# A two-layer GDN and HGRN2 flow step on one core: padded decay operands, token-tile order at the norms, key norms from the Gram diagonal, and a new plan

## The chip, the cores and the metric

The kernel runs on one core of a Trainium2 chip. The metric is the time of one execution on the device in microseconds (us). The time before is the median of three runs; the profile belongs to a fourth execution of the same kernel.

## The reference, cut to what matters

Two layers of a bidirectional backbone run on 128 prompt tokens and 256 sample tokens with D = 1024 and 8 heads of 128. Layer a mixes with a gated delta rule (GDN), layer b with HGRN2; after each mixer comes an MLP with 4096 hidden units. All weights and activations are fp32.

```
for layer in range(2):
    hmod = rms_norm(x, norm_g[layer, 0]) * (1 + sc1) + sh1
    mix  = gated_deltanet_mixer(hmod) if layer == 0 else hgrn2_mixer(hmod)
    x    = x + gt1 * rms_norm(mix, norm_g[layer, 1])
    hmod = rms_norm(x, norm_g[layer, 2]) * (1 + sc2) + sh2
    ff   = square(relu(hmod @ mlp_w1[layer])) @ mlp_w2[layer]
    x    = x + gt2 * rms_norm(ff, norm_g[layer, 3])

# inside the GDN mixer, per head, direction and chunk of 64 tokens
k      = k * rsqrt(sum(k * k) + 1e-6)
g      = cumsum(g)
decay  = exp(where(causal, g[i] - g[j], -inf))
lower  = (k * beta) @ k.T * decay * strict
tmat   = inverse(eye + lower)
u, w   = tmat @ (v * beta), tmat @ (k * beta * exp(g))
v_new  = u - w @ state
state  = state * exp(g_last) + (k * exp(g_last - g)).T @ v_new
```

sh1, sc1, gt1, sh2, sc2 and gt2 are six rows of silu(c) @ w_ada + b_ada, one set for the prompt and one for the sample.

## The kernel before, in words

The 384 tokens are three token tiles of 128: n = 0 is the prompt, n = 1 and 2 the sample. Activations stand transposed, 128 features by 384 tokens per tile. An fp32 product is made of three matmuls (`mm3`): both operands are split into a rounded high part and the rest, so every weight piece of 128x1024 goes through `split` (L1013): ACT writes wh, a rounded copy, and DVE writes wl, the difference. Both are in classes of three buffers. Matmuls go through the helper line L924, transposes through L930, DMAs through L941, DVE's tensor_tensor through L838, its scalar_tensor_tensor through L843, its tensor_scalar through L849, ACT's activations through L887 and its copies through L892, memsets through L856.

The order of the instructions is not that of the code. `Planner` (L540) records every operation with its unit (for instance d3 for the decay of head 3), and `run` (L625) then makes a list schedule of all five queues with estimated costs. The tables RESERVE, SHIFT, ADA and BUFS and the numbers SWITCH and WINDOW weight that choice; CAPS bounds the buffers of each class (L4, of tiles with up to 4 KB a row, has 9; L3, of 3 KB, has 4). A matmul whose operand shape differs from the one before is charged 85 ns there, a DMA 2000 ns of latency and its bytes at 320 per ns. Each engine then executes its list in order, and SP issues all DMAs in one order.

The steps that the change touches:

- **Gates and decays** (`gdn`, L1345, from the rows of `gp` on; `decay`, L1468). The cumulated log gates are cut into three bf16 parts (`gp`), stored to DRAM (`gd`) and loaded back into two tiles LH and RH of class L4 (tag LR), in rows 32n to 32n+5 for token tile n; the memsets of the two tiles give the ones and minus ones. `decay(h)` makes, for each of 8 heads and 3 token tiles, one PSUM tile of 128x256 out of three matmuls: maskb against identb (128 rows), then for both directions a product over 6 rows of LH and RH. ACT takes the exponential into `dec` (class L3), and one DMA stores the 384 KB of a head to `dd`.
- **Key norms** (`phase1`, L1504). The Gram matrix of a token tile's keys is in PSUM (pk). ACT squares the keys (k2), three matmuls against a column of ones (cst) give their sums, DVE's `c` and `iv` and POOL's `vsc` follow, and six DVE operations PU = pk * gam * dec give the matrix that `inverse` (L1536) inverts for four heads at a time. Four heads' PU go through DRAM (`du`) into the 31 steps of substitution and back (`dt`), and `merge` (L1579) puts 32x32 blocks together.
- **State step** (`vstep`, L1653). ACT writes w = py * gam out of PSUM, DVE multiplies w by a decay, and the product goes into the state matmul.
- **Borders.** `out_proj` (L1197, for both layers) and the last group of `w2` in `mlp` (L1284) accumulate three token tiles (acc) over pieces of the weights. `postnorm` (L1172) of a token tile follows when its last piece is in, then `prenorm` (L1147) of the next stage: ACT's sqj, POOL's rstd, DVE's pnt, x and xn, transposes (pj<-sml,xn), ACT's hhi and DVE's hlo, and only then the next stage's matmuls. In all of them the loop over pieces is outside the loop over token tiles.
- **First HGRN head** (`head`, L1760): its f and i products (pf) run over pieces outside, token tiles inside, too.

Other loads that run through the GDN stage are the rows of w_ada: ar (512 KB each, multiplied on TensorE into pad) and av (512 KB each, multiplied on DVE into avj with cvec, the broadcast condition).

Of the kernel before, what the change touches and what calls it, by code (L numbers as in the profile page):

```python
# [34 lines left out]
RESERVE = {'A32': 39,  # L35
 'A64': 69,
 'CR': 12,
 'HC': 5,
 'LR': 1,
 'PU': 16,  # L40
 'T64': 19,
 'Zs': 24,
 'ab': 15,
 'acc': 2,
 'adw': 0,
 'am': 25,
 'ar': 2,
 'atm': 56,
 'att': 7,
 'av': 2,  # L50
 'avj': 0,
 'ax': 3,
 'c1': 31,
 'cacc': 0,
 'cb': 3,
 'cbuf': 2,
 'crow': 42,
 'cvec': 2,
 'dec': 15,
 'dre': 20,  # L60
 'e1': 41,
 'gate': 4,
 'gp': 17,
 'gr': 10,
 'hE': 8,
 'hEn': 20,
 'hKD': 7,
 'hQD': 3,
 'hel': 27,
 'het': 2,  # L70
 'hf': 7,
 'hf0': 0,
 'hhi': 33,
 'hk': 15,
 'hlo': 23,
 'hsf': 5,
 'inv': 10,
 'iv': 33,
 'k0': 8,
 'k2': 0,  # L80
 'kT': 29,
 'ktt': 2,
 'lbo': 2,
 'lhl': 20,
 'mh': 29,
 'ml': 34,
 'mr': 8,
 'mst': 18,
 'nat': 2,
 'natr': 12,  # L90
 'of': 0,
 'ofl': 1,
 'oin': 45,
 'on': 64,
 'ors': 22,
 'osb': 0,
 'pad': 2,
 'pb': 2,
 'pf': 1,
 'pj': 2,  # L100
 'pm': 6,
 'pnt': 9,
 'po': 0,
 'qT': 1,
 'r': 42,
 'rstd': 32,
 'rsu': 34,
 's0': 3,
 's1': 73,
 'sf': 2,  # L110
 'sg': 16,
 'sqj': 0,
 'ss': 23,
 'ss2': 30,
 'sso': 37,
 'ssq': 28,
 'swt': 2,
 'tb': 1,
 'th': 3,
 'vT': 1,  # L120
 'vtt': 1,
 'w': 59,
 'w2': 61,
 'wh': 0,
 'wl': 0,
 'wr': 31,
 'x': 11,
 'xn': 28,
 'zl': 0,
 'zs': 3}  # L130
SWITCH = 862
TICK = 10240 / 3
WINDOW = 3068
SHIFT = {'aoh0': 4453,
 'aopn0': -32,
 'aopn1': -26,
 'aopn2': 55,
 'aow0': 3100,
 'aow1': -316,
 'aow2': 1579,  # L140
 'aow3': 201,
 'aow:ld': 826,
 'aow:sp': 2736,
 'apost0': 1380,
 'apost1': 184,
 'apost2': 4855,
 'apre0': 9298,
 'apre1': 6920,
 'apre2': 760,
 'awi0': 34,  # L150
 'awi1': -119,
 'awi2': 381,
 'awi3': 2862,
 'awi4': 1676,
 'awi5': 528,
 'awi6': 4228,
 'awi7': 770,
 'awi:ld': 3909,
 'awi:sp': 2021,
 'awo0': 5745,  # L160
 'awo1': 5025,
 'awo2': 14621,
 'awo3': 1449,
 'awo4': 4497,
 'awo5': 1510,
 'awo6': 1868,
 'awo7': 8060,
 'awo:ld': 5382,
 'awo:sp': 8906,
 'boh0': 3541,  # L170
 'bopn0': 5070,
 'bopn1': 3053,
 'bopn2': 4485,
 'bow0': -479,
 'bow1': -142,
 'bow2': 4668,
 'bow3': 10062,
 'bow:ld': 10903,
 'bow:sp': 2510,
 'bpost0': 318,  # L180
 'bpost1': -325,
 'bpost2': -72,
 'bpre0': 9493,
 'bpre1': 2181,
 'bpre2': 7646,
 'bwi0': -84,
# [1898 lines left out]
```

## Time and profile before

| | us |
|---|---|
| median of three runs | 1237.83 (1234.85 to 1239.44) |
| profiled execution | 1235.33 |
| its span | 1233.3 |
| PE busy | 1180.0 (96%) |
| DVE busy | 800.2 (65%) |
| ACT busy | 635.4 (52%) |
| POOL busy | 66.1 (5%) |
| moved by DMA | 207.82 MB |

The profiled execution is 2.50 us under the median, 0.2%. The mean granted clock of TensorE is 0.966 of full speed. Reading by stage: 0 to 87 us are the first norms, k projections and gates of layer a; 87 to 118 the decays; 118 to 176 projections beside the first inverse; 176 to 365 the merges, the heads' cores and the output projection; 390 to 650 the first MLP; 663 to 943 HGRN2; 962 to 1220 the second MLP. The short stretches between are the borders, where a norm stands between two products.

### The profile page before, as it was taken

What the parts mean: (1) busy time and instruction counts of PE and PEld (TensorE: products, weight loads), DVE (VectorE), ACT (ScalarE), POOL (GpSimd) and SP (SyncE); (2) the same over time, 40 slices, a digit from 0 to 9 for tenths busy, and PEclk for the clock granted to TensorE, in tenths of its full rate; (3) what the DMA queues carried; (4) which work ended last, traced back from release to release, by engine and by line L of the source; (5) the groups of instructions that cost most, each with busy time, mean ns of one, the idle gap of its engine ahead of it and who ended that gap; (6) DMA issues with size and microseconds to landing.
All of it is one profiled execution on the core that took longest, in us unless ns stands there. A gap on an engine that the chain in (4) does not pass through costs nothing.

```text
span 1233.3 us, 20383 instructions
## 1 busy us (share of the span) xinstructions
PE 1180.0 (96%) x7936; PEld 1047.6 (85%) x7936; DVE 800.2 (65%) x1578; ACT 635.4 (52%) x1283; POOL 66.1 (5%) x156
## 2 busy tenths in 40 slices
PE   6998998999998999999998999999998999999997
PEld 3775988888987998989988998888986999888986
DVE  4484878867999986666539967767666542333334
ACT  3383464775646643343436567674655564333442
POOL 1111001000002000000002000000002000000000
PEclk9996996899998999999998999999999999999999
DMA  9868771675353875556436642233432334233432
GB/s 359 318 248 281 225 214 33 198 248 186 119 182 134 302 237 191 192 184 205 152 115 205 210 150 97 76 110 111 159 133 84 107 137 137 103 127 118 138 129 86
DMA packets 82642, 207.82 MB, mean 169 GB/s; under 512 B 26058, under 2 KB 47842, under 8 KB 70514
## 3 DMA queue, kind: packets, MB, share of 16 engines
q1 hardware_dynamic: 82546, 206.53, 49.4%
q8 instruction: 62, 1.02, 0.3%
q14 instruction: 34, 0.28, 0.1%
HBM read 192.52 MB, written 13.99 MB: 167 GB/s over the span
## 4 chain that ended last, share of the span: by engine, by line
PE 60%; DVE 7%; ACT 5%; issue 2%; POOL 1%; POOLq 0%; DVEq 0%; ACTq 0%
PE acc L924 24%; PE pj L924 21%; PE pf L924 7%; PE nat L924 3%; PE pb L924 2%; PE po L924 1%; DVE wl L838 1%; ACT L887 1%; DVE A L838 1%; POOL rstd L838 1%; PE pb L930 1%; PE pj L930 1%; ACT wh L892 1%; DVE avj L843 1%; DVE hQD L838 1%
## 5 line engine op out<-in xcount | busy, mean ns | idle before, releaser
L838 DVE TENSOR_TENSOR wl<-wr,wh 128x1024 fp32r<-128x1024 f32 (+2 forms) x228 | 266.6, 1171 | 268.1 <-ACT wh L892 260.1
L892 ACT CAST wh<-wr 128x1024 fp32r<-128x1024 f32 (+2 forms) x228 | 230.3, 1010 | 403.8 <-PE pj L924 178.0
L924 PE MATMUL pj<-hhi,wh 128*128 128x384 f32 x800 | 272.5, 343 | 0.0
L924 PE MATMUL pj<-hhi,wl 128*128 128x384 f32 x800 | 271.1, 342 | 0.0
L924 PE MATMUL pj<-hlo,wh 128*128 128x384 f32 x800 | 270.9, 341 | 0.0
L924 PEld LDWEIGHTS pj<-hhi,wh 128*128 128x128 f32 x800 | 151.6, 190 | 2.4 <-issue 0.8
L924 PEld LDWEIGHTS pj<-hlo,wh 128*128 128x128 f32 x800 | 151.5, 190 | 1.8 <-issue 0.4
L924 PEld LDWEIGHTS pj<-hhi,wl 128*128 128x128 f32 x800 | 151.6, 190 | 1.4 <-DVE wl L838 0.5
L924 PE MATMUL acc<-wl,mh 128*128 128x512 f32 x384 | 149.5, 390 | 0.0
L924 PE MATMUL acc<-wh,ml 128*128 128x512 f32 x384 | 149.3, 390 | 0.0
L924 PE MATMUL acc<-wh,mh 128*128 128x512 f32 x384 | 145.4, 390 | 0.0
L843 DVE SCALAR_TENSOR_TENSOR avj<-av,cvec 128x1024 bf16<-128x1024 f32 x112 | 135.5, 1218 | 6.9 <-DMA dd<-dec 3.7
L924 PEld LDWEIGHTS acc<-wl,mh 128*128 128x128 f32 x384 | 72.1, 188 | 15.8
L924 PEld LDWEIGHTS acc<-wh,mh 128*128 128x128 f32 x384 | 72.1, 188 | 14.7
L924 PEld LDWEIGHTS acc<-wh,ml 128*128 128x128 f32 x384 | 72.1, 188 | 14.2
L924 PE MATMUL pf<-wh,hhi 128*128 128x384 f32 x192 | 63.6, 346 | 2.3 <-ACT hhi L892 2.3
L924 PE MATMUL pf<-wl,hhi 128*128 128x384 f32 x192 | 63.9, 342 | 0.1
L924 PE MATMUL pf<-wh,hlo 128*128 128x384 f32 x192 | 63.8, 345 | 0.0
L843 DVE SCALAR_TENSOR_TENSOR cacc<-cb,sml,cacc 128x392 f32<-128x392 f32 x96 | 58.9, 619 | 5.4 <-ACT cacc L887 4.5
L887 ACT ACT_TABLE_LOAD x35 | 44.9, 1283 | 3.6 <-DVE hk L849 2.4
L838 DVE TENSOR_TENSOR ml<-mr,mh 128x384 fp32r<-128x384 f32 x56 | 30.2, 554 | 14.7 <-PE acc L924 7.5
L924 PEld LDWEIGHTS pf<-wh,hhi 128*128 128x128 f32 x192 | 36.2, 190 | 2.9 <-ACT hhi L892 2.5
(255 smaller groups left out, 1898.0 us busy)
## 6 DMA issues: line engine op xcount, KB each, us to landing
wr<-in_w_dram SPq DMA_DIRECT2D x64, 1024.0 KB
av<-in_wv_dram SPq DMA_DIRECT2D x56, 512.0 KB
ar<-in_wa_dram SPq DMA_DIRECT2D x40, 512.0 KB
wr<-in_gq_dram SPq DMA_DIRECT2D x14, 1024.0 KB
wr<-in_hfi_dram SPq DMA_DIRECT2D x16, 768.0 KB
wr<-in_hqz_dram SPq DMA_DIRECT2D x8, 1024.0 KB
wr<-in_gout_dram SPq DMA_DIRECT2D x4, 1024.0 KB
wr<-in_hout_dram SPq DMA_DIRECT2D x4, 1024.0 KB
```

The lines of the kernel that those rows point to most:

```text
L838: self._go(lambda: self.r.tensor_tensor(fix(out), fix(in0), fix(in1), op), _n(out), [out], [in0, in1], rate, base=base)
L843: self._go(lambda: self.r.scalar_tensor_tensor(fix(out), fix(in0), fix(scalar), fix(in1), op0, op1, **{k: fix(v) for k, v in kw.items()}), ...
L887: self.pl.add("S", lambda: self.r.activation(fix(out), fix(in_), func, **{k: fix(v) for k, v in kw.items()}), cost, w, [x for x in (in_, b ...
L892: self.pl.add("S", lambda: self.r.copy(fix(out), fix(in_)), cost, [out], [in_])
L924: self.pl.add("PE", lambda: self.r.matmul(fix(out), lhsT=fix(lhsT), rhs=fix(rhs), start=start() if callable(start) else start, stop=stop, ...
L930: self.pl.add("PE", lambda: self.r.transpose(fix(out), fix(in_), fix(ident)), 111.0, [out], [in_, ident], geo=(4, 4))
```

## The change

**Decay operands.** LH becomes three tiles, one for each token tile, and RH one, all with 128 rows in class L4 (four buffers instead of two). Outside of its six rows an LH tile is zero; the decay matmul runs over all 128 rows. POOL makes seven memsets instead of two.

**Token-tile order.** `out_proj` for its second column half, a new `w2_last` for the last group of `w2`, and the first HGRN head's hfi split all four weight pieces first (`split4`; the fourth piece goes into class L4 under the tags xh and xl) and then finish token tile 0 over the whole sum, its postnorm, token tile 1, token tile 2.

**Key norms.** The sum of squares is read off the Gram matrix: one DVE scalar_tensor_tensor for each token tile multiplies pk by the identity and accumulates along the row. ACT's square and the three matmuls go. A product gam2 = gam * decay is made once for each head; in `vstep` DVE writes w2 = py * gam2 directly out of PSUM.

**Plan.** The shape change costs 160 ns instead of 85 in the planner, a DMA 2200 ns and its bytes run at 300 per ns; all tables are new. Class sm has four more real buffers, and two paddings (32 and 16 floats a row) stand in SBUF.

```diff
-RESERVE = {'A32': 39,
+RESERVE = {'A32': 55,
...
-SWITCH = 862
+GAP = 32
+SKEW = 16
+SWITCH = 1602
...
-                    st += 85.0
+                    st += 160.0
...
-                dma_free = max(dma_free, st + 2000.0) + op.dma
+                dma_free = max(dma_free, st + 2200.0) + op.dma
...
+    def split4(raws, shape):
+        out = []
+        for i in range(4):
+            extra = dict(cls=("L4", "L4"), tag=("xh", "xl")) if i == 3 else {}
+            out.append(split(raws[i // 2][:, 2 * (i % 2):2 * (i % 2) + 2], shape, **extra))
+        return out
...
+        pcs = split4([load(w[2 + kh], 4) for kh in range(2)], [128, 2, 512])
+        for n in range(NT):
+            pl.unit(f"{u}ow2")
+            pst[n][1] = ps("acc", 6)
+            for k in range(KC):
+                hi, lo = pcs[k // 2]
+                mm3(pst[n][1], hT["hi"][k][:, tsl[n]], hT["lo"][k][:, tsl[n]], hi[:, k % 2, :], lo[:, k % 2, :],
+                    k == 0, k == KC - 1)
+            pl.unit(f"{u}opn{n}")
+            postnorm(n, pst[n], x[n], gate)
...
+        def w2_last():
+            hh, hl = hbuf.pop(7)
+            pl.unit(f"{'ab'[l]}wo7")
+            pcs = split4([load(a["w2"][l, 14 + half], 4) for half in range(2)], [128, 2, 512])
+            for n in range(NT):
...
+                postnorm(n, [acc[n, 0], acc[n, 1]], x[n], gate, store)
...
-        LH = tl("L4", "LR", 2, [70, 16, 128], B16)
-        RH = tl("L4", "LR", 2, [70, 16, 128], B16)
-        G.memset(LH, 1.0, after=[p])
+        LH = [tl("L4", "LR", 4, [128, 16, 128], B16) for _ in range(NT)]
+        RH = tl("L4", "LR", 4, [128, 16, 128], B16)
         G.memset(RH, -1.0, after=[p])
         for n in range(NT):
             src = gd[:, :, tsl[n]].rearrange("r m t -> m r t")
-            DM.dma_start(out=LH[32 * n + 3:32 * n + 6], in_=src)
+            G.memset(LH[n], 0.0, after=[p])
+            G.memset(LH[n][32 * n:32 * n + 6], 1.0)
+            DM.dma_start(out=LH[n][32 * n + 3:32 * n + 6], in_=src)
...
-                    PE.matmul(px[:, c:c + 128], lhsT=LH[32 * n:32 * n + 6, d * 8 + h, :],
-                              rhs=RH[32 * n:32 * n + 6, d * 8 + h, :], start=False, stop=(d == 1))
+                    PE.matmul(px[:, c:c + 128], lhsT=LH[n][:, d * 8 + h, :], rhs=RH[:, d * 8 + h, :],
+                              start=False, stop=(d == 1))
...
-            k2 = tl("L1", "k2", 1, [128, T])
-            S.activation(k2, k, AF.Square)
-            pss = pb()
+            c1 = tl("sm", "c1", 2, [128, NT])
+            dj = tl("Lh", "dj", 1, [128, 128])
             for n in range(NT):
-                PE.matmul(pss[:, n:n + 1], lhsT=k2[:, tsl[n]], rhs=cst[:, C_ONE:C_ONE + 1], start=True, stop=True)
-            c1 = tl("sm", "c1", 2, [128, NT])
-            V.tensor_scalar(c1, pss[:, 0:NT], 1.0, EPS, ALU.mult, ALU.add)
+                V.scalar_tensor_tensor(dj, pk[:, tsl[n]], 1.0, ident, ALU.mult, ALU.mult, accum_out=c1[:, n:n + 1])
+            V.tensor_scalar(c1, c1, 1.0, EPS, ALU.mult, ALU.add)
...
-                    V.tensor_scalar(w2, w, EX[:, 2 + d, n, h:h + 1], None, ALU.mult)
+                    V.tensor_scalar(w2, py[:, 0:128], gam2[:, h, n, d:d + 1], None, ALU.mult)
```

How the order moves at three places. First SP's queue in the decay stage: dd is the store of a head's decays, ar and av are rows of w_ada, cvec the broadcast condition, adw and gt the result rows of w_ada, du the blocks for the inverse, s a state. Before, from the first dd on:

```order
L941 DMA dd<-dec_971 128x768
L941 DMA adw_1010<-in_adw_dram 128x512
L941 DMA ar_1020<-in_wa_dram 128x1024
L941 DMA gt_0_93<-adw_204 2x256
L941 DMA av_1033<-in_wv_dram 128x1024
L941 DMA cvec_1042<-cs 128x8x128
L941 DMA cvec_1051<-cs 128x8x128
L941 DMA dd<-dec_1065 128x768
L941 DMA dd<-dec_1084 128x768
L941 DMA av_1102<-in_wv_dram 128x1024
L941 DMA dd<-dec_1137 128x768
L941 DMA du_89<-PU_1002 32x12x32
```

And now:

```order
L952 DMA dd<-dec_972 128x768
L952 DMA dd<-dec_1000 128x768
L952 DMA ar_1027<-in_wa_dram 128x1024
L952 DMA gt_0_94<-adw_372 2x256
L952 DMA ar_1046<-in_wa_dram 128x1024
L952 DMA dd<-dec_1052 128x768
L952 DMA ar_1078<-in_wa_dram 128x1024
L952 DMA s_412_1093<-in_state_gdn_dram 128x2x128
L952 DMA dd<-dec_1080 128x768
L952 DMA du_90<-PU_996 32x12x32
L952 DMA gt_0_94<-adw_372 2x256
L952 DMA ar_1121<-in_wa_dram 128x1024
```

Both cvec and all av have left the space between the stores; some ar have come in.

Second POOL's list, from the last memset of the conv buffers (cb) before the decay operands (LR) to the first after them. Before:

```order
L856 MEMSET cb_117 128x5x2
L849 ISA
L849 TENSOR_SCALAR rsu_177<-ss_169 128x1
L838 TENSOR_TENSOR rstd_182<-rsu_177,nhalf 128x1
L849 TENSOR_SCALAR rsu_187<-ss_180 128x1
L838 TENSOR_TENSOR rstd_191<-rsu_187,nhalf 128x1
L849 TENSOR_SCALAR rsu_201<-ss_196 128x1
L838 TENSOR_TENSOR rstd_206<-rsu_201,nhalf 128x1
L856 MEMSET LR_630 70x2048
L856 MEMSET LR_649 70x2048
L856 MEMSET cb_725 128x2
```

And now:

```order
L867 MEMSET cb_198 128x5x2
L867 MEMSET LR_617 128x2048
L867 MEMSET LR_643 128x2048
L867 MEMSET LR_617 6x2048
L867 MEMSET LR_643 6x2048
L867 MEMSET LR_701 128x2048
L867 MEMSET LR_722 128x2048
L867 MEMSET LR_701 6x2048
L867 MEMSET cb_691 128x2
L867 MEMSET cb_691 128x5x2
```

Seven long memsets stand in one block ahead of the next conv buffers.

Third PE at the border from HGRN2's output projection to the second MLP: acc is the last accumulation of the projection, pj<-sml,xn a transpose of the normed tokens, nat the first product of the MLP. Before:

```order
L924 MATMUL acc_10201<-wh_10211,hlo_9865 128x512
L924 MATMUL acc_10201<-wh_10211,hhi_9861 128x512
L924 MATMUL acc_10201<-wl_10218,hhi_9861 128x512
L924 MATMUL acc_10201<-wh_10211,hlo_9865 128x512
L924 MATMUL pb_10298<-vtt_9298,het_9913 128x128 x2
L930 MATMUL pj_10303<-sml,xn_10256 128x128 x4
L924 MATMUL nat_10339<-wh_10239,hhi_10330 128x256
L924 MATMUL nat_10339<-wl_10261,hhi_10330 128x256
L924 MATMUL nat_10339<-wh_10239,hlo_10341 128x256
L930 MATMUL pj_10355<-sml,xn_10311 128x128 x4
```

And now:

```order
L935 MATMUL acc_10249<-wh_10168,hhi_9113 128x512
L935 MATMUL acc_10249<-wl_10178,hhi_9113 128x512
L941 MATMUL pj_10275<-sml,xn_10231 128x128 x4
L941 MATMUL pj_10280<-sml,xn_10231 128x128 x4
L935 MATMUL acc_10249<-wh_10168,hlo_9161 128x512
L935 MATMUL acc_10249<-wh_10168,hhi_9113 128x512
L935 MATMUL acc_10249<-wl_10178,hhi_9113 128x512
L935 MATMUL acc_10249<-wh_10168,hlo_9161 128x512
```

The transposes of token tile 0 now stand ahead of the last matmuls of the accumulation, not behind it.

## Rows read from the trace of the kernel before

**Rows 1.** Windows by stage: us, busy us of each engine (count), granted clock, DMA share, GB/s.

```profile
99.00:118.00 19.00, 15.93 (x75) 10.66 (x75) 10.82 (x31) 6.71 (x19) 3.32 (x5) 0.50 0.87 268
...
123.00:176.00 53.00, 53.00 (x319) 51.29 (x317) 47.26 (x118) 24.51 (x46) 1.14 (x5) 1.00 0.78 235
176.00:210.00 34.00, 28.49 (x402) 25.68 (x402) 24.25 (x68) 18.40 (x45) 2.07 (x6) 0.65 0.17 42
...
365.00:390.00 25.00, 19.69 (x98) 16.57 (x97) 23.93 (x44) 17.36 (x43) 7.71 (x17) 0.86 0.44 154
390.00:650.00 260.00, 260.00 (x1366) 237.54 (x1365) 173.23 (x241) 113.13 (x167) 1.32 (x6) 1.00 0.56 191
650.00:663.00 13.00, 9.06 (x43) 7.85 (x42) 12.11 (x26) 12.50 (x35) 7.55 (x14) 0.74 0.65 214
943.00:962.00 19.00, 13.51 (x68) 11.12 (x67) 17.56 (x32) 15.01 (x39) 7.83 (x16) 0.82 0.25 92
```

**Rows 2.** Timeline of PE in the decay stage: start, us, instruction, idle before and releaser.

```profile
87.12 0.28 PE L924 MATMUL pb<-maskb,identb 128*128 128x256 bf16 x1
...
87.55 0.28 PE L924 MATMUL pb<-maskb,identb 128*128 128x256 bf16 x1
...
105.11 0.37 PE L924 MATMUL pb<-maskb,identb 128*128 128x256 bf16 x1 [3.07 <-ACT dec L887]
...
118.15 0.67 PE L924 MATMUL pj<-hhi,wh 128*128 128x384 f32 x1
```

**Rows 3.** Waits between 87 and 118 us: waited for, us in total, times, longest.

```profile
ACT dec L887 <- DMA dd<-dec: 10.5, 3, 6.6
```

**Rows 4.** Timeline of SP's queue in the decay stage: issue, us, DMA.

```profile
90.53 0.33 SPq L941 DMA_DIRECT2D dd<-dec  x1
...
92.73 1.50 SPq L941 DMA_DIRECT2D cvec<-cs  x2
...
117.33 0.33 SPq L941 DMA_DIRECT2D dd<-dec  x1
```

**Rows 5.** DMA issues by group: count and KB each.

```profile
av<-in_wv_dram SPq DMA_DIRECT2D x56, 512.0 KB
...
dd<-dec SPq DMA_DIRECT2D x8, 384.0 KB
```

**Rows 6.** Tile LR, POOL's row: duration min/median/max ns, first and last start.

```profile
L856 POOL MEMSET LR<- x2: 1801/1802/1802, 54.1 to 55.9; 70x2048 bf16 x2
```

**Rows 7.** Timeline of DVE: two gate operations of one form, during and after those memsets.

```profile
56.97 0.90 DVE L849 TENSOR_SCALAR gr<-gr 64x384 f32<-64x384 f32 x1 [1.75 <-ACT gr L887]
...
64.52 0.42 DVE L849 TENSOR_SCALAR gr<-ax,nal 64x384 f32<-64x384 f32 x1
```

**Rows 8.** Timeline of PE at the last key norm, at full clock.

```profile
133.09 0.72 PE L924 MATMUL pb<-cst,k 128*128 128x1 f32 x6
```

**Rows 9.** Tile dec, DVE's row: duration ns min/median/max, first and last start.

```profile
L843 DVE SCALAR_TENSOR_TENSOR PU<-pb,gam,dec x24: 339/343/352, 90.1 to 107.5; 128x128 f32<-128x128 f32 x24
```

**Rows 10.** Tile w, ACT's row: the same columns.

```profile
L887 ACT ACTIVATE w<-pb,gam x48: 348/367/392, 195.2 to 352.8; 128x128 f32<-128x128 f32 x48
```

**Rows 11.** Timeline of PE at the three borders, the longest waits.

```profile
946.28 0.39 PE L924 MATMUL acc<-wh,hlo 128*128 128x512 f32 x1
946.50 0.39 PE L924 MATMUL acc<-wh,hhi 128*128 128x512 f32 x1
...
951.98 0.43 PE L924 MATMUL nat<-wh,hhi 128*128 128x256 f32 x1 [3.40 <-ACT hhi L892]
...
378.06 0.63 PE L930 MATMUL pj<-sml,xn 128*128 128x128 f32 x4 [4.04 <-DVE xn L849]
...
656.58 0.69 PE L924 MATMUL pf<-wh,hhi 128*128 128x384 f32 x1 [2.27 <-ACT hhi L892]
```

**Rows 12.** The costliest groups of instructions: weight splits, busy us, mean ns, idle before.

```profile
L838 DVE TENSOR_TENSOR wl<-wr,wh 128x1024 fp32r<-128x1024 f32 (+2 forms) x228 | 266.6, 1171 | 268.1 <-ACT wh L892 260.1
L892 ACT CAST wh<-wr 128x1024 fp32r<-128x1024 f32 (+2 forms) x228 | 230.3, 1010 | 403.8 <-PE pj L924 178.0
```

## Prediction before the run

> **What bounds the kernel now.** I read the windows by stage first. In the long products TensorE never pauses: 260.00 of 260 us in the first MLP, 53.00 of 53 beside the first inverse, at full clock [rows 1]. Only less work could shorten these stretches; the change takes none from the MLPs. The time to win stands in the short windows, and there in two columns, PE busy and granted clock. In 99 to 118 us, the decays, PE is busy 15.93 of 19 at a clock of 0.50, that is the lower of its two levels, 1.2 instead of 2.4 GHz; in 176 to 210, the first merges, 28.49 of 34 at 0.65; at the three borders 19.69 of 25, 9.06 of 13 and 13.51 of 19 at 0.86, 0.74 and 0.82 [rows 1].
>
> Second, the timeline of PE in the decay stage. The first decay group (maskb and two small products) starts at 87.12, the projections go on at 118.15: 31 us [rows 2] for 24 groups. Such a stage is not bound by PE: before the group at 105.11 PE stood 3.07 us waiting for ACT's dec [rows 2]. The waits say why ACT was late: its exponential waited 10.5 us, in three pieces and once 6.6, for the store dd<-dec to release a buffer [rows 3]. SP's queue says why the store was late: from the first store at 90.53 to the eighth at 117.33 [rows 4] stand, by the order of before, eight stores of 384 KB, five av, two ar and two cvec of 512 KB each, an adw of 256 KB and small ones: 8.3 MB (sizes from [rows 5] and, for ar, cvec and adw, from the shapes in the list). That in 26.8 us is 310 GB/s, where the windows show 268 in 99 to 118 [rows 1]. So the queue's bytes set the stage.
>
> Third, the borders: PE waits 4.04 us for xn, 2.27 for hhi and 3.40 for hhi in the longest pieces [rows 11]. What ends last there is the norm's chain of the first token tile, behind its accumulation.
>
> **The change part by part.** The sum is made against the profiled execution, 1235.33 us, 2.5 under the median.
>
> *Decay stage: −10.* In the new order the stores carry other company: between the first and the eighth stand four ar, one load of a state, one read-back dre of a head's decays (384 KB) and the du. With the eight stores that is 6.0 MB, 2.3 less; at 310 GB/s 7.4 us. The av and cvec still have to come, but into 123 to 176, where DMA is at a share of 0.78 [rows 1] and PE does not wait for it. I take −8. Padding: two groups in a row start 0.43 us apart [rows 2]; 512 columns take 0.22 us (two accumulation matmuls, 946.28 and 946.50 [rows 11]), so some 0.2 us of each group is change of shape, 5 us for 24. PE's waits cover most of it. What is left is that a denser stage may come back to the upper clock sooner: −2. Bounds: 0 (the inverse's or the projections' inputs are late anyway) and −18 (the waits, 10.5, go, and the half clock of 99 to 118 falls by most of its 9.5 us).
>
> *Start: −2.* By counting SP's lists, the eighth piece of the k weights stands behind 13.7 MB instead of 15.1. At the 268 GB/s of the window after [rows 1] 1.4 MB are 5 us; whether the start waits for loads to the end I can't tell, so bounds 0 and −5.
>
> *Key norms: −2 in all.* 48 matmul passes with one column go. Six of them took 0.72 us at full clock [rows 8], so 24 of them, for the four heads that lie in filled stretches, are 2.9 us; the other 24 lie in the decay stage, under its waits. ACT's eight squares go without effect; ACT has room. DVE gets 24 dj of the kind and size of PU, 0.343 us [rows 9], plus the read of an accumulator, so 9 to 10 us, and eight small products. DVE is busy 10.82 of 19 in the decays but 47.26 of 53 behind them [rows 1]. Four heads' 12 dj, some 5 us, stand on the way to the first inverse. That inverse is covered: PE has 53 us of projections. I charge +1; bounds 0 and +5.
>
> *State step: −1.* DVE's w2 no longer follows ACT's w of 0.367 us [rows 10]. Per step the serial chain loses a hop, but behind 250 us it is covered by projections. Only the first 8 steps, in the merges, can show it: 8 × 0.367 = 2.9 at best, 0 at worst.
>
> *POOL: +1.* Seven memsets of the 1.80 us kind [rows 6] replace two: 12.6 instead of 3.6 us in one block. Two conv buffers (cb_691, cb_727) stand behind them; DVE's convolutions for them may be late by up to 9 us, but the k projections ahead leave DVE other heads. Bounds 0 and +5. Here the trace speaks against the change in a second way: a gate operation on DVE that ran while POOL was setting LR took 0.90 us, its like behind the memsets 0.42 [rows 7]. The Trainium skill, "SBUF — State Buffer", section "Who interferes with whom", says that a DVE tensor_scalar or copy that takes both port pairs and a POOL instruction shut each other out for a whole instruction, the first to start winning. By that rule each such DVE operation in the block may lose up to a memset. That is a rival below.
>
> *Borders: −10.* Counting accumulation matmuls of 512 columns behind the last one of token tile 0, the lead of the first norm grows from 21 to 27 at the first border, from 24 to 36 at the second, from 25 to 45 at the third. At 0.227 us [rows 11] that is 1.4, 2.7 and 4.5 us more. The idle in the three windows is 5.3, 3.9 and 5.5; the lower clock costs about 25 × 0.14, 13 × 0.26 and 19 × 0.18, or 3.4 us each [rows 1]. The leads sum to 8.6. At the first border two avj that stood on DVE in the first norm's way are gone, and four small matmuls fill. I take −10; bounds 0 (the second token tile's chain is what waits next) and −25 (all idle and clock).
>
> *Splitting four pieces first: +1.* ACT takes 1.01 us and DVE 1.17 for a piece [rows 12]. In the new order some 15 matmuls stand between the first use of piece three and of piece four, 3.4 us; ACT needs one norm operation and the cast for it. It fits narrowly.
>
> *Paddings and the four small buffers: 0.* They add no instruction; no row tells what an address costs, and no engine waits for a buffer of class sm in the waits that I read.
>
> *New waits: +3.* A new plan leaves waits that its costs don't know. I take one of the size that the old one left, 3.07 [rows 2]; bounds −8 (merges: their idle and clock in 176 to 210 cost 5.5 and about 12) and +8.
>
> Sum: −10 −2 −2 −1 +1 −10 +1 +3 = −20, so 1215; I say 1216.
>
> **The rivals.**
>
> *A smaller gain.* The store waits go, but the first inverse, or POOL's block, then holds the merges: what is won at 118 us is idle in 176 to 210. For it: a clock of 0.65 there, so nothing covers. Against: the projections in between are worth 53 us. Only the borders and the norms pay: 1235 − 10 − 2 to 1235 − 4, so 1222 to 1231.
>
> *The port.* A DVE operation of the gates that starts under a memset ends with it. In the trace that cost 0.48 us once [rows 7]. If two of them each lose a whole memset of 1.80 us [rows 6], the first decay starts 3.6 us later, and every decay with it: about 1220. This is the case of the Trainium skill's rule named above.
>
> *A larger gain.* The decay stage keeps the upper clock (−9.5 of its half clock instead of −2) and the merges some of theirs (−5): about 1203.
>
> *No effect.* The padding and the token order do what they say, but another chain of equal length stands right behind each: hhi at the borders, where tile 0's xn was late before; the buffers of dec with ar in the queue instead of av. 1232 to 1244.
>
> *Slower: the four pieces.* At five places (two output projections, two ends of w2, the first HGRN head) no token tile can finish before the fourth piece is split. If the raw weights come just in time, PE stands for two pieces, 2 × (1.01 + 1.17) = 4.4 us [rows 12], five times: +22, and the borders win nothing: 1215 + 10 + 22 = 1247. It decides from the point where the fourth lo is ready later than about 4 us after PE has begun the third. Against it: DMA has a share of 0.25 to 0.65 at the borders [rows 1], so the weights lie there early.
>
> **How the numbers follow.** A measurement of this kernel can tell about 0.5% from no change, 6.2 us: faster is under 1231.6, slower over 1244. Forecast (1208 to 1222) 0.38; the port 0.05; smaller gain (1222 to 1231.6) 0.23; larger 0.12; no effect 0.13; slower 0.09. Faster is 0.78, same 0.13, slower 0.09. The range goes from 1198, under the larger gain, to 1240, into no effect; it leaves out 0.03 below and about 0.13 above.
>
> **What would show it.** Right: ACT's wait for dd<-dec under 4 us; 24 decay groups 0.25 us apart where they follow each other; projections resume within 23 us of the first group; the windows of the three borders together idle under 9 us instead of 14.7; PE's passes of cst,k gone and the stretch of projections still without a gap. Wrong: PE waits for wl or xl of the fourth piece at the ends of w2; a wait for inv or PU ahead of the merges that was 0.4 before and is several us now; decays that start after 90 us because POOL or the gates are late; dec still waiting for dd, behind ar.

## The result and the profile after

The changed kernel takes 1243.72 us (median of six runs, 1242.16 to 1246.13), the kernel before 1238.03 on the same measurement (six runs, 1234.55 to 1239.44). The ratio is 1.0053, 95% interval 1.0035 to 1.0071: some 6 us **slower**, where 20 us faster was forecast. The time lies outside the range given.

Where it was won and lost, read from the starts of PE's instructions in the two profiled executions ("ends" is the start of a stage's last accumulation matmul; the last column is a kernel of the experiments, e5, explained there):

| point, us from the span's start | before | after | difference | e5 |
|---|---|---|---|---|
| first decay group | 87.1 | 91.9 | +4.7 | 84.7 |
| projections go on | 118.2 | 114.8 | −3.4 | 107.7 |
| first merge | 176.4 | 173.8 | −2.6 | 166.2 |
| GDN's output projection ends | 373.6 | 365.9 | −7.7 | 358.3 |
| first MLP ends | 651.2 | 648.6 | −2.6 | 636.6 |
| HGRN2's output projection ends | 947.0 | 953.3 | +6.3 | 940.4 |
| span | 1233.3 | 1240.4 | +7.1 | 1224.6 |

So the decay stage gained 8 us and the rest of the GDN layer 4, but the start lost 5, HGRN2 lost 9 (the time between its two points, 304.7 us instead of 295.8) and the first MLP, in whose long products nothing was to change, lost 5.

The windows of the changed kernel over the stretches that answer to [rows 1], and over the start of layer a (us, busy us of PE, PEld, DVE, ACT and POOL with counts, granted clock, DMA share, GB/s):

```profile
60.00:70.00 10.00, 6.40 (x49) 4.84 (x48) 9.65 (x11) 7.85 (x13) 5.99 (x4) 0.97 0.89 348
70.00:80.00 10.00, 10.00 (x47) 9.45 (x47) 4.19 (x9) 4.38 (x10) 0.33 (x5) 0.52 0.48 161
...
92.00:114.00 22.00, 16.38 (x122) 9.49 (x121) 14.94 (x61) 13.69 (x34) 2.86 (x6) 0.84 0.75 251
...
173.00:210.00 37.00, 32.88 (x450) 30.19 (x447) 35.85 (x98) 22.67 (x62) 5.17 (x8) 0.77 0.59 208
366.00:378.00 12.00, 7.32 (x41) 5.78 (x40) 11.47 (x24) 10.63 (x29) 5.15 (x9) 0.86 0.24 87
...
649.00:661.00 12.00, 8.12 (x37) 7.07 (x38) 11.48 (x25) 11.07 (x29) 4.19 (x9) 0.72 0.46 153
...
953.00:965.00 12.00, 6.63 (x34) 5.45 (x33) 10.98 (x20) 8.95 (x21) 4.91 (x8) 0.72 0.25 89
```

The whole decay stage, before and after, has these windows:

```profile
87.10:118.10 31.00, 24.91 (x162) 15.01 (x161) 19.42 (x53) 16.91 (x42) 3.32 (x5) 0.69 0.90 290
```

```profile
91.90:114.80 22.90, 17.28 (x135) 10.37 (x131) 15.77 (x65) 14.59 (x36) 2.99 (x7) 0.85 0.76 255
```

So its clock is 0.85 instead of 0.69; the 0.50 of [rows 1] is the second part of the stage alone. But a stretch that had not been looked at, 70 to 80 us, stands at 0.52, the lower level, with PE busy all the time; and PE worked only 6.40 of the 10 us before it.

The timeline of PE in the decay stage of the changed kernel (start, us, instruction, idle before and its releaser) answers to [rows 2]:

```profile
91.86 0.28 PE L935 MATMUL pb<-maskb,identb 128*128 128x256 bf16 x1
...
103.20 0.28 PE L935 MATMUL pb<-maskb,identb 128*128 128x256 bf16 x1
...
103.44 0.27 PE L935 MATMUL pb<-maskb,identb 128*128 128x256 bf16 x1
...
103.66 0.27 PE L935 MATMUL pb<-maskb,identb 128*128 128x256 bf16 x1
...
114.78 0.42 PE L935 MATMUL pj<-hhi,wh 128*128 128x384 f32 x1
```

From first group to projections 22.9 us instead of 31.0, groups that follow each other 0.23 us apart instead of 0.43. The waits of ACT there (us in total, times, longest) answer to [rows 3]:

```profile
ACT dec L898 <- DMA dd<-dec: 2.2, 1, 2.2
```

A wait of ACT's dec for DVE's PU, 2.8 us, is new there. And SP's queue, to [rows 4]: eight stores in 18.5 us instead of 26.8.

```profile
96.39 1.17 SPq L952 DMA_DIRECT2D dd<-dec  x2
...
114.91 0.32 SPq L952 DMA_DIRECT2D dd<-dec  x1
```

Up to here the prediction's working holds. What it did not have shows in three other views. First DVE's timeline beside POOL's memsets of LR, whose row (duration min, median, max in ns, first and last start) stands first:

```profile
L867 POOL MEMSET LR<- x7: 1794/1805/1898, 53.5 to 68.2; 128x2048 bf16 x4, 6x2048 bf16 x3
```

```profile
58.91 1.95 DVE L860 TENSOR_SCALAR gr<-gr 64x384 f32<-64x384 f32 x1
...
65.22 3.15 DVE L860 TENSOR_SCALAR gr<-ax,nal 64x384 f32<-64x384 f32 x1
```

In [rows 7] the same operation, undisturbed, took 0.42. PE waited for the second of them, and after that wait the clock of the window above went to its lower level:

```profile
68.51 0.52 PE L941 MATMUL pb<-sml,gr 128*128 128x128 f32 x3 [3.60 <-DVE gr L860]
```

Second, the pace of the products. PE's timeline of the kernel before, in the second MLP, where nothing waits:

```profile
1009.76 0.33 PE L924 MATMUL pj<-hhi,wl 128*128 128x384 f32 x1
...
1012.88 0.33 PE L924 MATMUL pj<-hhi,wl 128*128 128x384 f32 x1
```

and of the changed one:

```profile
1013.80 0.34 PE L935 MATMUL pj<-hhi,wh 128*128 128x384 f32 x1
...
1016.97 0.34 PE L935 MATMUL pj<-hhi,wh 128*128 128x384 f32 x1
```

Between the two rows of either kernel lie 18 steps from one matmul to the next: 3.12 us before, 173 ns a step; 3.17 after, 176 ns. Same instruction, same clock, no idle, 3 ns more. There are 2,400 pj products of this shape alone, so 2,400 × 3 ns, some 7 us.

Third, HGRN2. DVE's groups of instructions in that stage (busy us, mean ns, idle before), in the kernel before

```profile
L843 DVE SCALAR_TENSOR_TENSOR avj<-av,cvec 128x1024 bf16<-128x1024 f32 x16 | 19.2, 1218 | 0.1
```

and in the changed one

```profile
L854 DVE SCALAR_TENSOR_TENSOR avj<-av,cvec 128x1024 bf16<-128x1024 f32 x48 | 57.8, 1213 | 0.1
```

The new plan has put 32 of the 112 avj, 39 us of DVE, into the stage in which DVE makes the operands that PE waits for.

### The profile page after: what moved, and what is told of

The parts are those of the page before. It is cut to its first block, busy times and chain, and to the rows that moved or that the text cites. A ratio compares the mean times of both kernels' runs of the same rounds, so it can differ in the third digit from the quotient of the medians.

```text
span 1240.4 us, 20287 instructions
## 1 busy us (share of the span) xinstructions
PE 1182.0 (95%) x7888; PEld 1045.4 (84%) x7888; DVE 806.7 (65%) x1634; ACT 638.6 (51%) x1277; POOL 79.4 (6%) x161
## 4 chain that ended last, share of the span: by engine, by line
PE 73%; DVE 13%; ACT 7%; issue 4%; POOL 2%; DMA 1%; SPq 0%; POOLq 0%; DVEq 0%; ACTq 0%
PE pj L935 29%; PE acc L935 26%; PE pf L935 5%; PE pb L935 5%; PE nat L935 3%; DVE avj L854 2%; DVE wl L849 2%; PE k L935 1%; PE pad L935 1%; DVE cacc L854 1%; PE po L935 1%; PE pb L941 1%; ACT L898 1%; DVE A L849 1%; ACT wh L903 1%
## 5 line engine op out<-in xcount | busy, mean ns | idle before, releaser
L849 DVE TENSOR_TENSOR wl<-wr,wh 128x1024 fp32r<-128x1024 f32 (+2 forms) x223 | 260.4, 1170 | 285.0 <-ACT wh L903 284.7
L903 ACT CAST wh<-wr 128x1024 fp32r<-128x1024 f32 (+2 forms) x223 | 224.5, 1009 | 367.1 <-PE acc L935 168.7
L935 PE MATMUL acc<-wl,mh 128*128 128x512 f32 x372 | 146.4, 395 | 0.0
L935 PE MATMUL acc<-wh,ml 128*128 128x512 f32 x372 | 146.1, 395 | 0.2 <-DVE ml L849 0.2
L935 PE MATMUL acc<-wh,mh 128*128 128x512 f32 x372 | 142.2, 395 | 0.0
L860 POOL TENSOR_SCALAR ss<-ss 128x1 f32<-128x1 f32 x21 | 8.1, 384 | 549.0 <-ACT sqj L898 540.0
L849 POOL TENSOR_TENSOR ors<-e,nhalf 128x3 f32<-128x3 f32 x16 | 20.2, 1261 | 350.8 <-DVE e L860 270.2
```

Of the source, the lines that this page charges most:

```text
L849: self._go(lambda: self.r.tensor_tensor(fix(out), fix(in0), fix(in1), op), _n(out), [out], [in0, in1], rate, base=base)
L860: self._go(lambda: self.r.tensor_scalar(*[fix(x) for x in args]), _n(out), [out], [in0, s1, s2], rate, base=None if self.e == "V" else 160 ...
L903: self.pl.add("S", lambda: self.r.copy(fix(out), fix(in_)), cost, [out], [in_])
L935: self.pl.add("PE", lambda: self.r.matmul(fix(out), lhsT=fix(lhsT), rhs=fix(rhs), start=start() if callable(start) else start, stop=stop, ...
```

## The experiments

The theory after this reading: the mechanism of the decays works; the loss is (a) the place of the buffers in SBUF, by the padding GAP, (b) DVE's gate operations under POOL's memsets, (c) avj in HGRN2. The rivals: the loss comes from the new order as a whole, or from the borders.

**e1, e2: each padding alone.** GAP stands ahead of the weight pieces, SKEW in another place.

```diff
-GAP = 32
+GAP = 0
```

> The changed kernel with GAP = 0: no 32 floats of padding ahead of the class wh, so that the weight pieces stand at a multiple of 6144 bytes from the activations, as before. Layout theory: in the changed kernel a product of 384 columns is issued every 176 ns instead of 173.4 and one of 512 columns every 232.5 instead of 227.6, in 3096 and 1536 of them 14 to 15 us in all, and the cause is this padding. Then the pitch goes back to 173 and 227 ns and the time to about 1229. Order theory (the pitch is a matter of what the other engines and the DMA do beside PE in the new order): pitch and time stay, 1243 to 1245. Noise of layout theory: class sm also moves behind the activations, which should cost nothing.

1234.51 us, ratio to before 0.9979 (0.9967 to 0.9990): 9.2 us less than the changed kernel. The pace came back as the layout theory says (the mean of acc<-wl,mh is 391 ns, in the changed kernel 395), but the size missed: the theory said 1229, from the steps saved times the number of products, and where the other 5 us went was not traced.

```diff
-SKEW = 16
+SKEW = 0
```

> The changed kernel with SKEW = 0 and GAP = 32: the base of the pool goes 64 bytes down, the padding ahead of wh stays. If the distance between weights and activations sets the pitch, nothing changes: 1242 to 1246, 384 columns in 176 ns. If the absolute address (the base of the pool) sets it, the pitch goes back to 173 ns and the time to about 1229.

1243.67 us, 1.0047 (1.0030 to 1.0064): SKEW has no effect that these runs can tell. The 32 floats of GAP cost 9 us, without one instruction more.

**e3: the same padding in the kernel before.**

```diff
+        PAD = 32
...
+    if t["cls"] == "wh" and PAD:
+        pool.tile([128, PAD], F, tag="pad", bufs=1, name="gap")
+        PAD = 0
```

> The kernel before with nothing but the 32 floats of padding ahead of class wh. Layout theory: its pitch rises from 173.4 to about 176 ns and from 227.6 to about 232 ns, and the time by 14 us to about 1252. Order theory: no change, 1236 to 1240.

A miss: 1236.76 us, 0.9997 (0.9984 to 1.0011). The reason lies in `Planner.add`, which lists an operation's tiles in the order of a Python set of names; their buffers are opened in that order. The first operation that needs both a tile of class sm and one of class L6 (the activations hhi, hlo, mh, ml) so decides by chance which region lies first. The buffers' sizes give what follows. One of the two operands of each of these products is an activation, the other a weight piece wh or wl. From an activation buffer to the weight pieces the distance within a row of SBUF is, modulo 512 bytes, in the kernel before 0 or 384, by that chance; in the changed one 128 in either case (with four more, the 48 sm buffers of 32 bytes are 1536, a multiple of 512, and GAP adds its 128 bytes). That the distance was 0 in the kernel before, and in e3 384 + 128 = 512, that is 0 too, is inferred from their times and their pace (390 ns in the rows below). The next three kernels fix that order (`touched` a dict, sorted by class) and choose the distance.

**e6, e10, e12: the distance chosen.** e6 is the kernel before with sm first and 32 floats of padding (128), e12 the kernel before without padding but with L6 first (384), e10 the changed kernel with GAP 64 (256).

```diff
-        touched = set()
+        touched = {}
...
-                touched.add(name)
+                touched[name] = True
...
-        for name in touched:
+        for name in sorted(touched, key=lambda n: n in self.tile_of and self.tile_of[n]["cls"] == "sm", reverse=True):
```

> The kernel before, with its plan, with 32 floats of padding ahead of the weight class and the two regions in a fixed order, so that weights and activations surely stand 128 bytes past a multiple of 512 apart (in the earlier run with the padding alone the order of the two regions was left to chance, and with the other order the distance is a multiple of 512). Distance theory: the pitch is now 175 to 177 ns instead of 173.4 for 384 columns and about 232 instead of 227.6 for 512, and the time 8 to 10 us longer, 1245 to 1248. Order theory (the pitch comes with the new plan, and GAP = 0 only shifted something else): pitch 173 and 227, 1235 to 1240.

> The changed kernel with 64 floats of padding instead of 32, regions in fixed order: weights and activations 256 bytes past a multiple of 512 apart. If only a multiple of 512 is free of the loss: pitch 175 to 177 and 232 ns, 1242 to 1246. If the loss belongs to odd multiples of 128 bytes: pitch 173 and 227, about 1234.

> The kernel before with its plan and without padding, the two regions in the other fixed order: 44 buffers of 32 bytes of class sm stand between activations and weights, so the distance is 384 bytes past a multiple of 512. If only a multiple of 512 is free of the loss, the pitch is 175 to 177 and 232 ns and the time 1244 to 1248: then the kernel before has a slow layout too, left to chance. If the loss belongs to 128 alone: 1235 to 1240.

| kernel | distance mod 512 | us | ratio to before |
|---|---|---|---|
| before | 0 | 1236.8 to 1238.7 | |
| e6, before | 128 | 1246.06 | 1.0074 (1.0057 to 1.0091) |
| e12, before | 384 | 1246.28 | 1.0066 (1.0049 to 1.0083) |
| after | 128 | 1243.72 | 1.0053 (1.0035 to 1.0071) |
| e1, after | 0 | 1234.51 | 0.9979 (0.9967 to 0.9990) |
| e10, after | 256 | 1235.19 | 0.9972 (0.9956 to 0.9988) |

The groups of PE's instructions, shapes kept apart (busy us, mean ns of one, idle before), show the same in one row of each kernel. Before:

```profile
L924 PE MATMUL acc<-wl,mh 128*128 128x512 f32 x384 | 149.5, 390 | 0.0
```

e3, which by its pace has 0 too:

```profile
L928 PE MATMUL acc<-wl,mh 128*128 128x512 f32 x384 | 149.4, 390 | 0.0
```

e12, the program of before with 384:

```profile
L924 PE MATMUL acc<-wl,mh 128*128 128x512 f32 x384 | 151.2, 395 | 0.0
```

e6, the same program with 128 bytes between:

```profile
L928 PE MATMUL pj<-hhi,wl 128*128 128x384 f32 x800 | 273.2, 344 | 0.0
...
L928 PE MATMUL acc<-wl,mh 128*128 128x512 f32 x384 | 151.2, 395 | 0.0
```

After:

```profile
L935 PE MATMUL pj<-hhi,wl 128*128 128x384 f32 x800 | 270.3, 342 | 0.0
...
L935 PE MATMUL acc<-wl,mh 128*128 128x512 f32 x372 | 146.4, 395 | 0.0
```

e10, after with 256 bytes:

```profile
L935 PE MATMUL pj<-hhi,wl 128*128 128x384 f32 x800 | 267.6, 339 | 0.0
...
L935 PE MATMUL acc<-wl,mh 128*128 128x512 f32 x372 | 144.9, 390 | 0.0
```

At 0 and 256 a 512-column matmul takes 390 ns, at 128 and 384 it takes 395; a 384-column one of the changed order takes 339 against 342. So odd multiples of 128 bytes between the two operands cost 8 to 9 us here, in both orders of the program. It is the distance and not one address: e6 moves the weight pieces and leaves the activations where they are in the kernel before, e12 moves the activations and leaves the weight pieces, and both are slow. And the kernel before is fast by chance: e12 is a layout that its own source may take, and it is no faster than the changed kernel. The Trainium skill, "TensorE: Matmul & The Clock Gate", section "Step-by-step: what each phase is for", says that TensorE has independent read ports for the moving operand and for the weight load, so that loading the next weights takes no read bandwidth from the running matmul. Whether that is the whole of it here is open: with everything else equal the pace goes with the distance between the two, 390 ns or 395. That the two reads meet in the memory is a guess; no run shows whether they meet, or in what.

**e4: the gate operations in a form with two inputs.** The constant and the scalar become operands of stride 0; memsets and order stay.

```diff
-        V.tensor_scalar(gr[0:64], gr[0:64], 0.5, 0.5, ALU.mult, ALU.add)
+        half = sub(phalf[0:64], 0, [[0, T]])
+        V._go(lambda: V.r.scalar_tensor_tensor(fix(gr[0:64]), fix(gr[0:64]), 0.5, half, ALU.mult, ALU.add), T,
+              [gr[0:64]], [gr[0:64]], 0.521)
...
-        V.tensor_scalar(gr[hh], ax[hh], nal[hh], None, ALU.mult)
+        nalb = sub(nal[hh], 0, [[0, T]])
+        V._go(lambda: V.r.tensor_tensor(fix(gr[hh]), fix(ax[hh]), nalb, ALU.mult), T, [gr[hh]],
+              [ax[hh], nal[hh]], 0.521, scal=(nal[hh],))
```

> The changed kernel with its two gate operations gr on DVE (64x384) written as operations with two tensor inputs (the constant read with stride 0), same plan and same costs in the plan. Port theory: they took 1.95 and 3.15 us because POOL was setting the decay operands; as two-input operations they take about 0.56 us each under the same memsets, PE's wait of 3.60 us for gr at 68.5 goes, the half clock from 69.4 to 79.6 (5 us) goes with it, and the time falls by 8 us to about 1235. Rival (the gates are not on the path, the stage is bound by loads or by the memsets, whose last ends at 70.1): gr is short, but the first decay still starts at 92 and the time falls by 0 to 3 us, 1240 to 1244. Rival (no port, DVE is slow for another reason): gr stays long, no change.

1238.59 us, 1.0001 (0.9990 to 1.0013): 5.1 less than the changed kernel by the medians, some 6 by the ratios to before, not 8. DVE's timeline of e4:

```profile
59.56 0.54 DVE L1447 SCALAR_TENSOR_TENSOR gr<-gr,phalf 64x384 f32<-64x384 f32 x1
...
65.88 0.56 DVE L1458 TENSOR_TENSOR gr<-ax,nal 64x384 f32<-64x384 f32 x1
```

its PE there

```profile
66.58 0.52 PE L941 MATMUL pb<-sml,gr 128*128 128x128 f32 x3 [0.98 <-DVE gr L1458]
```

and its windows

```profile
70.00:80.00 10.00, 10.00 (x88) 8.13 (x85) 8.25 (x32) 7.54 (x15) 3.56 (x15) 1.00 0.69 231
...
359.00:376.00 17.00, 12.53 (x64) 10.87 (x64) 15.11 (x34) 11.99 (x30) 5.31 (x9) 0.70 0.23 78
948.00:965.00 17.00, 11.64 (x63) 10.42 (x62) 13.74 (x25) 9.83 (x22) 5.17 (x8) 0.70 0.19 63
```

Under the same seven memsets the two operations take 0.54 and 0.56 us; PE's wait falls from 3.60 to 0.98 and the lower clock of 70 to 80 us is gone. The first decay starts at 85.81 instead of 91.86. So the port, a rival of the prediction by the Trainium skill's rule ("SBUF — State Buffer", "Who interferes with whom"), did act, and the trace agrees with that rule: the single-input form is blocked while POOL only writes, the two-input form is not. Of the 6 us won at the decays 5.1 remain in the median and 3.3 in the profiled execution (span 1237.1 instead of 1240.4): the granted clock at the first and the third border is lower in it (0.70 over 17 us in both, against 0.90 and 0.80 over equal stretches of the changed kernel). Why it is lower there was not tried.

**e5: both.** GAP 0 with the order of the regions fixed, and e4's edit.

> The changed kernel with both repairs, GAP = 0 and the gate operations with two inputs; the order in which class sm and the class of the activations get their regions is now fixed by the code (sm first), so that weights and activations surely stand a multiple of 512 bytes apart. If the two causes are separate they add: 9.2 us and 5.1 us off 1243.7, about 1229.5, faster than before by 0.6%. If they overlap (the later stretches swallow what the earlier win): 1232 to 1235.

**1227.18 us, 0.9919 (0.9904 to 0.9933): 10 us faster than the kernel before, 16.5 faster than the changed one.** Its points are the last column of the first table: it leads by 15 us at the end of the GDN layer and gives 8 back in HGRN2. This is the version to keep. The next four kernels take it as their base.

**e9: decay products on six rows again**, everything else of e5 kept (`cut` takes these rows of both operands).

```diff
-                              start=False, stop=(d == 1))
+                              start=False, stop=(d == 1), cut=slice(32 * n, 32 * n + 6))
```

> The kernel with both repairs, same plan and same memsets, but each decay product takes only its six rows of LH and RH again, so each group changes the operand shape twice. Theory (a shape change costs some 0.1 us and the stage is now dense enough to feel it): groups that follow each other start 0.43 us apart instead of 0.22, the stage from the first group (84.8) to the first projection behind it gets longer, and the time rises by 2 to 5 us against the kernel with both repairs. Rival (the waits for ACT's dec and for adw still cover it): the stage and the time stay within 1 us, and the shorter queue of stores alone carries what the stage won.

1232.72 us, 0.9948 (0.9934 to 0.9963): 5.5 more than e5 by the medians, some 4 when each is set against the kernel before measured beside it (1238.71 here, 1237.21 beside e5). PE's timeline of e9 has the groups 0.43 us apart,

```profile
100.28 0.28 PE L935 MATMUL pb<-maskb,identb 128*128 128x256 bf16 x1
...
100.71 0.28 PE L935 MATMUL pb<-maskb,identb 128*128 128x256 bf16 x1
```

and its window from the first group to the projections is 28.2 us long at a clock of 0.70:

```profile
85.40:113.60 28.20, 24.76 (x135) 10.39 (x131) 16.21 (x67) 15.35 (x36) 3.48 (x7) 0.70 0.68 226
```

e5's is 23.0 us long at 0.85:

```profile
84.70:107.70 23.00, 17.37 (x133) 10.42 (x130) 15.70 (x66) 14.80 (x36) 2.86 (x6) 0.85 0.76 260
```

ACT's wait for the stores is 1.8 us in e9 and 2.3 in e5. So with short waits for the stores in both, the stage is 28.2 us on six rows and 23.0 on full rows: of the 8 us of this stage some 5 are the padding's. The other 3 are left for the company of the stores and whatever else is new in the stage; no run separates these.

**e8: HGRN2's output projection in the old loop order**, pieces outside, token tiles inside, split two by two; all else of e5 kept.

```diff
+        if l == 1:
+            for half in range(2):
+                pcs = []
+                for kh in range(2):
...
+                    raw = load(w[half * 2 + kh], 4)
+                    pcs += [split(raw[:, 2 * j:2 * j + 2], [128, 2, 512]) for j in range(2)]
...
+                    for n in range(NT):
...
+                        if half == 1 and kh == 1:
+                            pl.unit(f"bopn{n}")
+                            postnorm(n, pst[n], x[n], gate)
```

> The kernel with both repairs, in which the second layer's output projection has the old loops (pieces outside, token tiles inside, no fourth piece in class L4); the plan up to about 880 us is the same. Theory (a longer lead of the first norm takes idle off the border): PE's idle between the projection and the second MLP, 5.4 us in the repaired layout, rises by the lead lost, up to 4.5 us, and the time by 2 to 5 us against the kernel with both repairs. Rival (the second and third token tiles' chains set the border, the lead only moves the wait): under 1 us either way.

1232.04 us, 0.9968 (0.9952 to 0.9983): 4.9 more than e5. PE's waits at that border in e8:

```profile
945.35 0.58 PE L935 MATMUL nat<-wh,hhi 128*128 128x256 f32 x1 [2.53 <-ACT hhi L903]
...
950.68 1.11 PE L941 MATMUL pj<-sml,xn 128*128 128x128 f32 x4 [2.94 <-DVE xn L860]
```

and in the changed kernel, with one more row of the kernel before behind it:

```profile
954.24 0.38 PE L935 MATMUL nat<-wh,hlo 128*128 128x256 f32 x1 [0.22 <-DVE hlo L849]
958.43 1.11 PE L941 MATMUL pj<-sml,xn 128*128 128x128 f32 x4 [3.81 <-DVE xn L860]
960.89 2.82 PE L941 MATMUL pj<-sml,xn 128*128 128x128 f32 x12 [1.34 <-DVE xn L860]
```

```profile
953.83 1.11 PE L930 MATMUL pj<-sml,xn 128*128 128x128 f32 x4 [0.35 <-DVE xn L849]
```

The token order does hide the first tile's chain: the 3.40 us of [rows 11] for hhi are gone. The second tile's xn is late in its place, by 3.81 where the trace of before has 0.35 for it. e8 has this order undone under the new plan, so its 4.9 us say what the order is worth in this plan, not what it gave against the kernel before.

**e7, e11: fewer avj in HGRN2.** They cut 32 avj (rows sh2 and sc2 of the second layer) and 48 (gt1 too) to 64 of their 1024 columns, and so leave most of these sums out. The edit of e11:

```diff
+                if (l, kind) in ((1, "gt1"), (1, "sh2"), (1, "sc2")):
+                    V._go(lambda s=skip, r=raw, c=cb[m], w=v[:, m, k:k + 1]: V.r.scalar_tensor_tensor(
+                        fix(s[:, :64]), fix(r[:, :64]), 1.0, fix(c[:, :64]), ALU.mult, ALU.mult, accum_out=fix(w)), 1024,
+                          [skip, v[:, m, k:k + 1]], [raw, cb[m]], 1.042, extra=62.0)
+                    continue
```

> The kernel with both repairs, same plan, in which the 32 DVE products avj for the second layer's sh2 and sc2 take 64 of 1024 columns (these modulation rows are left wrong: most of their sum is left out). In the new plan 48 avj of 1.2 us, 58 us, stand in the HGRN2 stage, before 16; that stage (from the end of the first MLP's accumulation to that of its output projection) takes 303.7 us in the repaired layout against 295.8 before, with DVE busy 254 us against 218. Theory (DVE's queue delays HGRN2): the stage falls to about 298 and the time by 5 to 6 us against the kernel with both repairs. Rival (the stage is longer because of PE's own order and shape changes): under 1.5 us.

> The kernel with both repairs, same plan, in which all 48 DVE products avj for the second layer's gt1, sh2 and sc2 take 64 of 1024 columns (these rows are left wrong: most of their sum is left out). With 32 of them cut the HGRN2 stage went from 303.8 to 300.4 us. If DVE's queue is the whole of the 8 us by which the stage is longer than before: the stage falls to 296 to 298, the time to 1220 to 1222. If the rest is the order of PE itself: it stays at 299 to 300, the time at 1222 to 1224.

1223.47 us (0.9890, 0.9875 to 0.9904) and 1221.93 (0.9866, 0.9851 to 0.9881): 3.7 and 5.3 less than e5 by the medians (e11 some 7, each set against the kernel before measured beside it). Windows of the stage in e5

```profile
637.00:940.00 303.00, 290.52 (x2371) 256.20 (x2372) 253.29 (x556) 185.04 (x372) 18.58 (x29) 0.99 0.48 163
```

and in e11

```profile
637.00:940.00 303.00, 290.30 (x2375) 258.49 (x2375) 211.70 (x561) 187.19 (x377) 19.39 (x32) 0.99 0.48 163
```

With DVE at 211.70 us, below the 217.62 that the kernel before has in 651 to 947, the stage from the end of the first MLP to the end of the output projection takes 300.0 us (300.4 in e7). Before it was 295.8, in e5 303.8. So the avj are 3.8 of the 8 us. The other 4 stay open, and DVE's load in all does not explain them. PE stands idle for 12.5 us of this stage in e5, for 10.4 in e11 and for 7.1 before: TensorE's matmuls there are nearly the same in number, its waits are for operands that DVE and ACT make (the largest group after the border's is po<-DVE atm, in e5 six waits of 1.6 us in all, before two of 0.7 in all), and which piece of the new order makes them late was not separated.

## Why the prediction was wrong

Step by step, by the prediction's own parts.

- **"Paddings and the four small buffers: 0" is the step that failed most.** "They add no instruction; no row tells what an address costs" was true and should have given a bound, not a zero. Measured: +9 (e1 against the changed kernel; e6 and e12 against before, +8 to +9): nothing waits, and still a 512-column matmul takes 395 ns instead of 390. Nothing in a trace of one layout could have shown it; but the change names two paddings, and a part of a change whose effect no row prices needs both ends in the range.
- **The port was named, and priced too low.** The rival had 3.6 us and a chance of 0.05. The two operations lost 1.5 and 2.7 us, 4.3 together; what it had left out is the clock: PE's wait for gr of 3.60 us was followed by ten us at the lower level. Together 5.1 (e4). Of "POOL: +1" nothing else was seen. "Start: −2" is right once that is away: 84.7 in e5 against 87.1.
- **Decay stage, −10: measured −8.1** in the changed kernel, and −8.0 in e5. The waits for the stores fell as said, from 10.5 to 2.2. The shares were wrong: I gave the queue 8 and let PE's waits cover most of the padding's 5. e9 gives the padding some 5 in this stage and 4 to 5.5 in the kernel. Shape changes lie on the path there, because each group is what ACT waits for next, and the slower stage also spends more of its time at the lower clock.
- **Key norms −2, state step −1, and the merges among the "new waits".** From the first merge to the end of GDN's output projection 192.1 us instead of 197.2, in the changed kernel and in e5 alike. The new DVE operation takes 0.286 us and 0.082 for the accumulator's read, against 0.343 and a read that were assumed. What of the 5 us is whose was not tried.
- **Borders, −10: measured some −3.** PE is idle in the three windows for 4.68 + 3.88 + 5.37 = 13.9 us, against 14.7 before; the forecast of under 9 fell. The lower clock costs 12 × 0.14 + 12 × 0.28 + 12 × 0.28 = 8.4, against some 10 before. The rival "no effect" had the mechanism: another chain of equal length stands right behind the first. DVE is busy 11.47 of 12, 11.48 of 12 and 10.98 of 12 us in these windows, so I read DVE's queue as what a longer lead can't shorten; no run took DVE's load away there.
- **New waits, +3: HGRN2 took +8.** The reserve was sized by a wait in the decay stage, and looked for at the merges. I had compared the order at the places of the change, not the work per stage: a count of avj per stage on DVE, 16 before and 48 after, was to be had from the order without a run.
- **The four pieces did not decide.** At the first HGRN head, the one place where PE waits for a piece's lo, it stood 0.33 us, not 4.4. "+1" is not contradicted.

Added up from runs, the stages as e5 has them: the buffers' distance +9, the port +5, HGRN2 +8 (3.8 of it avj, 4 open), the start without the port −2, the decay stage −8, the middle of GDN −5, and −1 in the two MLPs. That is +6, as measured; what the borders gave is contained in these stages.

## What to carry to other kernels

Whoever adds or removes a buffer moves all that lie behind it: compare the steps of the plainest matmul in a stretch without waits in both traces before reading anything else (a mean over the whole kernel can hide them: that of pj<-hhi,wl is 342 ns in both traces here), and choose the distance between the two operands on purpose rather than leave it to an allocation order. A long memset on POOL belongs where DVE has no single-input operation that TensorE waits for, or the DVE operation gets a second input. Where a planner makes a new order, count each engine's work by stage, also for the operations that the change doesn't name.

## What the runs showed of the hardware that was not expected

- A matmul's pace depends on the distance between its two operands in SBUF. With 0 or 256 bytes modulo 512, steps of 173 ns (384 columns) and a mean of 390 ns (512 columns); with 128 or 384, 176 and 395. No other row of the trace shows it: no idle, no wait, the same clock.
- A 64x384 tensor_scalar of 0.42 us took 1.95 and 3.15 us beside memsets of 1.80: the second lost more than one whole memset.
- One wait of PE of 3.60 us stood ahead of a stretch at the lower clock level (0.52 in 70 to 80 us, so some 4.8 us of these ten) that cost more than the wait; with a wait of 0.98 in its place (e4) that stretch was at 1.00.
